# Mean over the rows of an 8192 x 8192 matrix: VectorE additions replaced by fp32 matmuls on four TensorE column tiles, with 4 MB loads on two DMA queues

## The chip, the cores and the metric

The kernel runs on one core of one Trainium2 chip. Its time is the time on the device, in microseconds; each number called a time is the median of several runs. A profile is one execution recorded by the hardware profiler; its span runs from the first to the last instruction.

## The reference

The input is a matrix of 8192 rows and 8192 columns in fp32, 268.4 MB. The output has 8192 elements, the mean of each column:

```python
def reference(x: np.ndarray) -> np.ndarray:
    return np.mean(x, axis=0)
```

There is one addition for each element read, and almost nothing is written.

## The kernel before, in words

The rows lie on the 128 partitions: a row tile is 128 consecutive rows, and there are 64 of them (`n_rt`). The columns are cut into four blocks of 2048 (`CB`, `n_cb`). One load brings one block of one row tile, 128 rows of 8 KB, 1 MB in all.

All loads are issued by SyncE, on its DMA queue, in the order of the loops: row tile by row tile, and in each the four column blocks. The pool `ld` has eight buffers of 1 MB, so up to eight loads are in flight or waiting to be used. The first four loads (line 35) go to the list `firsts`; from row tile 1 on, each load (line 42) is followed by one addition on VectorE. For row tile 1 the addition writes `firsts + t` into one of four accumulators `accs` of 128 x 2048 (line 44); for the other 62 row tiles it adds `t` to the accumulator in place (line 46). So VectorE makes 252 additions of 128 x 2048 fp32 elements, and a buffer is free for the next load when its addition is done.

After that, each accumulator holds 128 partial sums per column. They are summed over the partitions with TensorE: `ones` is a column of 128 elements with the value 1/8192, and `ones.T @ accs` gives a row of 512 means in a PSUM bank (line 52). There are 16 such matmuls, four for each column block. VectorE copies each row from PSUM to SBUF (line 53), and SyncE stores each finished block of 2048 means (line 54). These three lines stand after the loops over the row tiles.

The loads are thus made of rows of 8 KB because a block is 2048 columns wide; in memory a row of the matrix is 32 KB without a gap.

The order of work is that of the program on each engine; a framework puts in the waits between engines (a load waits until its buffer is free, an addition waits for its load, and so on). An fp32 matmul call shows in the trace as two MATMUL instructions, each with a weight load (LDWEIGHTS) of its own.

Of the kernel before, what the change touches and what calls it, by code (L numbers as in the profile page):

```python
# [1 line left out]

# [4 lines left out]


@with_exitstack
def kernel(  # L10
    ctx: ExitStack,
    tc: tile.TileContext,
    x: bass.AP,
    out: bass.AP,
):
    nc = tc.nc
    M, N = x.shape
    P = nc.NUM_PARTITIONS
    CB = 2048
    n_cb = (N + CB - 1) // CB  # L20
    n_rt = (M + P - 1) // P
    FREE = nc.PSUM_BANK_SIZE_BYTES // 4

    with tc.tile_pool(name="ld", bufs=8) as ld, \
         tc.tile_pool(name="acc", bufs=1) as accp, \
         tc.tile_pool(name="sg", bufs=1) as sg, \
         tc.tile_pool(name="psum", bufs=4, space=bass.MemoryType.PSUM) as psp, \
         tc.tile_pool(name="res", bufs=2) as resp:
        ones = sg.tile([P, 1], mybir.dt.float32)
        nc.any.memset(ones[:], 1.0 / M)  # L30
        accs = [accp.tile([P, CB], mybir.dt.float32, name=f"acc{i}") for i in range(n_cb)]
        firsts = []
        for cb in range(n_cb):
            t0 = ld.tile([P, CB], mybir.dt.float32)
            nc.sync.dma_start(out=t0[:], in_=x[0:P, cb * CB:(cb + 1) * CB])  # L35
            firsts.append(t0)
        for ri in range(1, n_rt):
            r0 = ri * P
            for cb in range(n_cb):
                c0 = cb * CB  # L40
                t = ld.tile([P, CB], mybir.dt.float32)
                nc.sync.dma_start(out=t[:], in_=x[r0:r0 + P, c0:c0 + CB])  # L42
                if ri == 1:
                    nc.vector.tensor_add(out=accs[cb][:], in0=firsts[cb][:], in1=t[:])  # L44
                else:
                    nc.vector.tensor_add(out=accs[cb][:], in0=accs[cb][:], in1=t[:])  # L46
        for cb in range(n_cb):
            c0 = cb * CB
            r = resp.tile([1, CB], mybir.dt.float32)
            for fi in range(0, CB, FREE):  # L50
                ps = psp.tile([1, FREE], mybir.dt.float32)
                nc.tensor.matmul(out=ps[:], lhsT=ones[:], rhs=accs[cb][:, fi:fi + FREE])  # L52
                nc.vector.tensor_copy(out=r[:, fi:fi + FREE], in_=ps[:])  # L53
            nc.sync.dma_start(out=out[c0:c0 + CB], in_=r[:1, :])


# [1 line left out]
_INS = ['x']  # L58
_OUTS = [((8192,), 'float32')]


# [23 lines left out]
```

## Time and profile before

| what | value |
|---|---|
| time, median of 3 runs | 659.93 us (659.87 to 660.07) |
| span of the profiled execution | 658.1 us |
| VectorE busy | 587.1 us, 268 instructions |
| TensorE busy (matmul) | 17.0 us, 32 instructions |
| loads | 256 of 1024 KB, issued by SyncE, median 17.5 us from issue to landing |
| read from HBM | 268.44 MB, 408 GB/s over the span |

The profile of the execution gives its span; the runs' times also contain what lies around it, 1.83 us by the difference of the two numbers above. Engines are named PE (TensorE matmul), PEld (TensorE weight load), DVE (VectorE), ACT (ScalarE), POOL (GpSimd) and SP (SyncE). `L46` is line 46 of the listing. A row of a group reads: line, engine, operation, output <- input with their shapes, then the count, the busy time in us, the mean of one in ns, and after the bar the idle time before these instructions and what ended it. In the chain that ended last, a row is start (us from the span's start), duration, and what it was. In a row of windows, each engine has its busy time and number of instructions in that stretch, then follow the clock that TensorE was granted, the mean busy share of the 16 DMA engines, and what they moved in GB/s. `q1` is the queue that carries the loads and stores; `q14` brings the engines their instructions.

### The profile page before, as it was taken

The numbers are of one execution on the slowest core, as the hardware profiler recorded it, in microseconds if no ns is written. First come the engines' busy times: TensorE is split into PE (matmuls) and PEld (weight loads), VectorE is DVE, ScalarE is ACT, GpSimd is POOL, SyncE is SP. The second block draws the span as 40 slices with busy tenths as digits, with TensorE's granted clock in tenths as the row PEclk, the third lists the DMA queues.
The fourth block names the chain that finished last, engine by engine and source line by source line (L and its number), as shares of the span: only waits on it lengthen the run. The fifth ranks groups of instructions, "written<-read, shape, count | busy, mean of one in ns | idle before, by whom it ended". The sixth has DMA issues, their size and how long they took to land.

```text
span 658.1 us, 1142 instructions
## 1 busy us (share of the span) xinstructions
PE 17.0 (3%) x32; PEld 2.8 (0%) x32; DVE 587.1 (89%) x268; POOL 0.3 (0%) x5
## 2 busy tenths in 40 slices
PE   0000000000000000000000000000000000000028
PEld 0000000000000000000000000000000000000001
DVE  0999989999999998999999999899999999899997
POOL 0000000000000000000000000000000000000000
PEclk9999999999999999999999999999999999999999
DMA  8999999999999999999999999999999999999980
GB/s 366 422 422 422 422 421 421 421 423 421 422 422 422 422 421 421 421 422 422 422 422 422 422 422 422 419 422 421 421 422 422 422 422 422 421 421 421 422 349 2
DMA packets 36880, 268.55 MB, mean 408 GB/s; under 512 B 4100, under 2 KB 4100, under 8 KB 4100
## 3 DMA queue, kind: packets, MB, share of 16 engines
q1 hardware_dynamic: 36872, 268.48, 98.1%
q14 instruction: 8, 0.07, 0.0%
HBM read 268.44 MB, written 0.03 MB: 408 GB/s over the span
## 4 chain that ended last, share of the span: by engine, by line
DMA 85%; DVE 12%; PE 1%; issue 1%; SPq 0%; DVEq 0%
DMA t<-in_x_dram 85%; DVE acc L46 12%; PE ps L52 1%; DVE acc L44 0%; DVE r L53 0%; SPq L35 0%; DVEq L46 0%; SPq L42 0%; DVEq L44 0%
## 5 line engine op out<-in xcount | busy, mean ns | idle before, releaser
L46 DVE TENSOR_TENSOR acc<-acc,t 128x2048 f32<-128x2048 f32 x248 | 568.0, 2292 | 51.4 <-DMA t<-in_x_dram 51.4
L52 PE MATMUL ps<-acc,ones 128*1 128x512 f32 x32 | 17.0, 691 | 638.0 <-DVE acc L46 637.9
L44 DVE TENSOR_TENSOR acc<-t,t 128x2048 f32<-128x2048 f32 x4 | 9.2, 2292 | 16.1 <-DMA t<-in_x_dram 16.1
L53 DVE COPY r<-ps 1x512 f32<-1x512 f32 x16 | 10.3, 673 | 1.0 <-PE ps L52 0.9
L52 PEld LDWEIGHTS ps<-acc,ones 128*1 128x1 f32 x32 | 2.8, 91 | 651.2 <-issue 646.5
L69 POOL MEMSET const-bfloat16-1.0<- 128x1 bf16 x1 | 0.1, 101 | 0.0
L69 POOL MEMSET const-uint8-127<- 128x1 uint8 x1 | 0.1, 101 | 0.0
L30 POOL MEMSET ones<- 128x1 f32 x1 | 0.1, 98 | 0.3 <-POOLq L69 0.3
L69 POOL MEMSET const-float32-0.0<- 128x1 f32 x1 | 0.1, 98 | 0.2 <-issue 0.2
L69 POOL MEMSET const-float32-1.0<- 128x1 f32 x1 | 0.1, 98 | 0.0
## 6 DMA issues: line engine op xcount, KB each, us to landing
t<-in_x_dram SPq DMA_DIRECT2D x256, 1024.0 KB, 17.5
out_dram<-r SPq DMA_DIRECT2D x4, 8.0 KB
```

The costliest lines, as they stand in the source:

```text
L30: nc.any.memset(ones[:], 1.0 / M)
L44: nc.vector.tensor_add(out=accs[cb][:], in0=firsts[cb][:], in1=t[:])
L46: nc.vector.tensor_add(out=accs[cb][:], in0=accs[cb][:], in1=t[:])
L52: nc.tensor.matmul(out=ps[:], lhsT=ones[:], rhs=accs[cb][:, fi:fi + FREE])
L53: nc.vector.tensor_copy(out=r[:, fi:fi + FREE], in_=ps[:])
L69: nc = _bacc.Bacc("TRN2", target_bir_lowering=False, num_devices=1)
```

## The change

All additions move from VectorE to TensorE. `ones` becomes a block of 128 x 32 with the value 1/8192. The 8192 columns of a row tile are cut into 16 pieces of 512; each piece is multiplied with `ones` and accumulated in PSUM over all 64 row tiles. Four PSUM banks hold the sums (`NB` = 4). In each bank a piece has 32 of the 128 partitions, all 32 with the same sums, and the matmul that writes it uses the column tile of TensorE at the same place: 128 rows by 32 columns of the array (`tile_position=(0, 32 * q)`). The program goes through the four column tiles in turn.

A load is now a whole row tile, 128 rows of 32 KB, 4 MB. The pool `ld` has five such buffers. Even row tiles are issued by SyncE, odd ones by ScalarE, each on its own DMA queue.

The last row tile is loaded in seven pieces by SyncE, into buffers of its own: three of 1 MB, one for each of the first three banks, and four of 256 KB (runs of 512 B) for the last bank. When a bank has its last matmul, VectorE copies the bank (128 x 512) to SBUF and ScalarE stores one partition of each group of 32.

The core of the diff:

```diff
-    CB = 2048
-        ones = sg.tile([P, 1], mybir.dt.float32)
-                nc.sync.dma_start(out=t[:], in_=x[r0:r0 + P, c0:c0 + CB])
-                    nc.vector.tensor_add(out=accs[cb][:], in0=accs[cb][:], in1=t[:])
-                nc.tensor.matmul(out=ps[:], lhsT=ones[:], rhs=accs[cb][:, fi:fi + FREE])
-                nc.vector.tensor_copy(out=r[:, fi:fi + FREE], in_=ps[:])
-            nc.sync.dma_start(out=out[c0:c0 + CB], in_=r[:1, :])
...
+    F = 512
+    NB = N // (4 * F)
+    n_rt = M // P
+    SPL = 128
...
+    ld = ctx.enter_context(tc.tile_pool(name="ld", bufs=5))
+    lastp = ctx.enter_context(tc.tile_pool(name="lastp", bufs=1))
...
+    ones = sg.tile([P, 32], f32)
+    nc.vector.memset(ones[:], 1.0 / M)
+    banks = [psp.tile([P, F], f32, name=f"bank{b}") for b in range(NB)]
+
+    def mm(b, q, c0, w, rhs, start, stop):
+        nc.tensor.matmul(
+            out=banks[b][32 * q:32 * q + 32, c0:c0 + w],
+            lhsT=ones[:],
+            rhs=rhs,
+            start=start,
+            stop=stop,
+            tile_position=(0, 32 * q),
+            skip_group_check=True,
+        )
+
+    for ri in range(n_rt - 1):
+        t = ld.tile([P, N], f32)
+        (nc.sync if ri % 2 == 0 else nc.scalar).dma_start(out=t[:], in_=x[ri * P:(ri + 1) * P, :])
+        for b in range(NB):
+            for q in range(4):
+                c = (b * 4 + q) * F
+                mm(b, q, 0, F, t[:, c:c + F], ri == 0, False)
+
+    r0 = (n_rt - 1) * P
+    out_v = out.rearrange("(b q c) -> b q c", b=NB, q=4)
+    x_v = x.rearrange("r (b q c) -> r b q c", b=NB, q=4)
+    for b in range(NB - 1):
+        t = lastp.tile([P, 4, F], f32, name=f"last{b}")
+        nc.sync.dma_start(out=t[:], in_=x_v[r0:r0 + P, b])
+        for q in range(4):
+            mm(b, q, 0, F, t[:, q, :], False, True)
+        r = resp.tile([P, F], f32, name=f"r{b}")
+        nc.vector.tensor_copy(out=r[:], in_=banks[b][:])
+        nc.scalar.dma_start(out=out_v[b], in_=r[0:128:32, :])
+    b = NB - 1
+    r = resp.tile([P, F], f32, name=f"r{b}")
+    for s in range(F // SPL):
+        t = lastp.tile([P, 4, SPL], f32, name=f"lasts{s}")
+        nc.sync.dma_start(out=t[:], in_=x_v[r0:r0 + P, b, :, s * SPL:(s + 1) * SPL])
+        for q in range(4):
+            mm(b, q, s * SPL, SPL, t[:, q, :], False, s == F // SPL - 1)
+    nc.vector.tensor_copy(out=r[:], in_=banks[b][:])
+    nc.scalar.dma_start(out=out_v[b], in_=r[0:128:32, :])
```

More of the change, by code (lines that the diff above doesn't have):

```diff
@@ L16 @@
     nc = tc.nc
+    f32 = mybir.dt.float32
     M, N = x.shape
     P = nc.NUM_PARTITIONS
-    CB = 2048
[L20 to L28, printed above, removed]
-        ones = sg.tile([P, 1], mybir.dt.float32)
[L30 to L41, printed above, removed]
-                nc.sync.dma_start(out=t[:], in_=x[r0:r0 + P, c0:c0 + CB])
[L43 to L53, printed above, removed]
-            nc.sync.dma_start(out=out[c0:c0 + CB], in_=r[:1, :])
@@ new lines @@
+    F = 512
[4 more added lines that the diff above has]
+    lastp = ctx.enter_context(tc.tile_pool(name="lastp", bufs=1))
+    sg = ctx.enter_context(tc.tile_pool(name="sg", bufs=1))
+    psp = ctx.enter_context(tc.tile_pool(name="psum", bufs=1, space=bass.MemoryType.PSUM))
+    resp = ctx.enter_context(tc.tile_pool(name="res", bufs=1))
+    ones = sg.tile([P, 32], f32)
+    nc.vector.memset(ones[:], 1.0 / M)
+    banks = [psp.tile([P, F], f32, name=f"bank{b}") for b in range(NB)]
```

## The prediction

> **What bounds the kernel now.** I read the page first (engines, slices, packets), then the chain in order of time, then windows over the last 20 us.
>
> ```profile
> span 658.1 us, 1142 instructions
> ...
> DMA  8999999999999999999999999999999999999980
> ...
> DMA packets 36880, 268.55 MB, mean 408 GB/s; under 512 B 4100, under 2 KB 4100, under 8 KB 4100
> ...
> q1 hardware_dynamic: 36872, 268.48, 98.1%
> q14 instruction: 8, 0.07, 0.0%
> ...
> DMA 85%; DVE 12%; PE 1%; issue 1%; SPq 0%; DVEq 0%
> L46 DVE TENSOR_TENSOR acc<-acc,t 128x2048 f32<-128x2048 f32 x248 | 568.0, 2292 | 51.4 <-DMA t<-in_x_dram 51.4
> L52 PE MATMUL ps<-acc,ones 128*1 128x512 f32 x32 | 17.0, 691 | 638.0 <-DVE acc L46 637.9
> ```
>
> The 16 DMA engines are full until the last two slices. VectorE is busy for 568 us, but what it idles for is the next load. The stream sets the time, then an end in which no load runs. The pace of the stream:
>
> ```profile
> 600.47 17.47 DMA t<-in_x_dram
> ...
> 618.02 2.30 DVE acc L46
> ...
> 620.35 17.48 DMA t<-in_x_dram
> ```
>
> A load of eight in flight takes 17.47 us, and the next on the same buffer starts 19.88 after the one before: 2.485 us per 1 MB. Four stretches of the chain, 160 us apart, are longer:
>
> ```profile
> 79.98 18.12 DMA t<-in_x_dram
> ...
> 239.66 18.43 DMA t<-in_x_dram
> ...
> 399.66 18.43 DMA t<-in_x_dram
> ...
> 559.72 18.45 DMA t<-in_x_dram
> ```
>
> They exceed 17.47 by 0.65 + 0.96 + 0.96 + 0.98 = 3.55 us. The page has 8 packets of instructions, two for each of these; I take them as the cause. What they leave is seen where the stream ends:
>
> ```profile
> core 0: us, PE busy (x) PEld busy (x) DVE busy (x) POOL busy (x), PEclk, DMA share, GB/s
> 637.00:638.00 1.00, 0.14 (x1) 0.11 (x2) 0.81 (x2) 0.00 (x0) 1.00 1.04 434
> 638.00:639.00 1.00, 1.00 (x2) 0.13 (x1) 1.00 (x1) 0.00 (x0) 1.00 0.48 197
> 639.00:640.00 1.00, 1.00 (x2) 0.13 (x1) 1.00 (x1) 0.00 (x0) 1.00 0.12 49
> 641.00:642.00 1.00, 1.00 (x2) 0.13 (x1) 1.00 (x1) 0.00 (x0) 1.00 0.10 41
> 642.00:644.00 2.00, 2.00 (x4) 0.34 (x3) 2.00 (x3) 0.00 (x0) 1.00 0.00 0
> 656.68:656.70 0.02, 0.00 (x0) 0.00 (x0) 0.00 (x0) 0.00 (x0) 1.00 0.03 0
> ```
>
> One engine moves 1 MB / 16 per 2.485 us, 26.4 GB/s, so 49 GB/s are two engines: two of 16 work on for three microseconds after the rest, as if each fetch always falls to the same engine of its queue. The stream is over at about 642.3.
>
> ```profile
> 15.52 2.29 DVE L44 TENSOR_TENSOR acc<-t,t 128x2048 f32<-128x2048 f32 x1 [15.52 <-DMA t<-in_x_dram]
> ...
> 654.97 0.68 DVE L53 COPY r<-ps 1x512 f32<-1x512 f32 x1 [0.18 <-PE ps L52]
> ```
>
> The first add needs five loads: 15.52 - 5 x 2.485 puts the start at 3.1. Check: 3.1 + 256 x 2.485 + 3.55 = 642.8. After the stream come 15.8 us of matmuls and copies in turn; from the end of the last copy (655.65) to the end of the span, 2.45. The median of the runs, 659.93, is 1.83 above the profiled span; I keep that.
>
> **The stream after the change.** Each engine now moves, per 4 MB, 8 rows of 32 KB and one small completion packet, where it moved 32 rows of 8 KB and four (the 4100 small packets are 256 x 16 and 4). The last window above holds only the completion packet of the last store: 3% of 16 engines x 0.02 us is 9.6 ns, nearly all of it fixed cost. If each packet carries that, a row tile saves (24 + 3) x 9.6 = 0.26 us: 9.94 becomes 9.68, and 63 tiles take 609.8. If rows are still cut at 8 KB, only the three small packets go, 0.03 per tile. I take the first: before, too, a row of the tile was one packet. The last row tile: three loads of 1 MB, 7.46, and four of 256 KB in runs of 512 B. A run is a sixteenth of a packet's bytes ((2485 - 9 x 9.6) / 8 / 16 = 18.7 ns) + 9.6; 32 of them and a completion make 0.92, four 3.7. Sum: 3.1 + 609.8 + 7.5 + 3.7 = 624.0, before fetches.
>
> The second queue shares the same engines, and the share is at 1.0 already, so I give it nothing. SyncE issues 39 transfers in place of 260, ScalarE, otherwise idle, 35. A load that waits for its buffer has only later loads of its queue behind it, and four others are in flight: 0, as long as TensorE is less than three tiles (29 us) behind. The 252 adds vanish; they lay beside the stream: 0.
>
> **Fetching TensorE's program.** This part is new. A call of matmul is four instructions (16 calls: 32 MATMUL and the weight loads below). The changed kernel has 63 x 16 + 12 + 16 = 1036 calls, 4144 instructions. 1142 instructions went with 8 packets, 143 each, so 29 packets. What one costs the path: 3.55 / 8 = 0.44 us, if both fetches of a stretch delay the same engine; 0.89, if each has its own, as the two late engines say; 0, if TensorE's fetches spread over 16 engines. I take 0.44, the mean of the ends and the price per packet that the path shows, since a second data queue may fill part of the gap: 12.8 us. SyncE's and VectorE's own 3.55 go (few instructions are left there); the 624.0 does not hold them.
>
> [...]
>
> **TensorE's pace.**
>
> ```profile
> 641.23 0.13 PEld L52 LDWEIGHTS ps<-acc,ones 128*1 128x1 f32 x1 [0.73 <-issue]
> 642.08 0.13 PEld L52 LDWEIGHTS ps<-acc,ones 128*1 128x1 f32 x1 [0.73 <-issue]
> ...
> 644.22 0.08 PEld L52 LDWEIGHTS ps<-acc,ones 128*1 128x1 f32 x1 [0.34 <-issue]
> 644.65 0.08 PEld L52 LDWEIGHTS ps<-acc,ones 128*1 128x1 f32 x1 [0.34 <-issue]
> ```
>
> Half a matmul takes 0.85 us for the first six microseconds, then 0.43 (the clock column says 1.00 throughout; I go by the pace). So 0.86 per call, 13.7 per row tile of 16: over the 9.7 of its load. All hangs on overlap between the column tiles, which nothing here shows. In program order, the second half of a call waits for the first on its tile, and the next call's first half can run beside it: two at a time, 0.43 per call, 6.9 per row tile. All four at once: 3.4. Either hides under the stream. I take the pairs, since the halves come in order in the rows.
>
> [...]
>
> **The end.** Two queues that take turns on each engine land two tiles together: 60 and 61, then 62, then the last row. From the first landing TensorE has 16 x 3 + 12 + 4 = 64 calls' work, 27.5 us, and 3 more for its slow start; the stream has one tile and the last row, 9.7 + 11.2, and a fetch: 21.3. So TensorE ends 9.2 after the stream (0.9 with four at once). Then wait and copy (0.18 + 0.68, the same 512 columns) and 2.45: 3.3.
>
> **Forecast.** 624.0 + 12.8 + 9.2 + 3.3 = 649.3; + 1.8 = 651 us, 1.3% faster. Its own range, with a fetch at 0.3 to 0.7 and either overlap, is 639 to 658.
>
> **The rivals.**
> - Fetches cost nothing on the path, because they spread over the engines or fall into gaps: 624.0 + 9.7 + 3.3 + 1.8 = 639, down to 630 with four column tiles at once. For it: TensorE fetched nothing during the stream of this trace, so its own way of fetching is not shown. Against: both engines that did fetch paid. 0.23. [...]
> - Slower: one DMA engine carries all of TensorE's fetches at 0.89, 25.8 us; every load waits for that engine. 624.0 + 25.8 + 8.8 + 3.3 + 1.8 = 664. It decides against the change from (658.1 - 624.0 - 12.5) / 29 = 0.74 us per packet. For it: the two late engines; against: in front of two queues the gap may be smaller. 0.20.
> - Rows still go in 8 KB pieces: 14.5 us come back, 666. 0.08.
> - The change does not do what it says, the column tiles run one after another: 64 x 13.7 from 22.5 (two tiles landing together) with a slow start and the end is about 909. 0.11.
>
> **How the numbers follow.** The forecast has 0.36; 0.02 is left for turns between two queues costing time, which one queue cannot show. A measurement here tells 0.2% (1.3 us) from no change. Faster: the forecast but for its edge, and the first rival, 0.57. Same: the edges of forecast and second rival, 0.06. Slower: the rest, 0.37. The range 630 to 667 leaves out the serial case, the queue turns and the outer ends.
>
> **What would show it.** Packets: a mid-stream rate of about 430 GB/s (4.19 MB per 9.68 us), and 63 x 128 = 8064 packets of 32 KB. Fetches: q14 with some 29 more packets, and near the end of the stream windows at 26 or so GB/s, one engine alone, for 10 us or more. Overlap: row tiles' matmuls 6.9 us apart in warm stretches (3.4 or 13.7 refute it). The end: a last wait of the copy on TensorE, not on a load. A share of DMA under 0.95 in mid-stream would make the whole sum wrong: then the buffers, hence TensorE, set the pace.

## The result, and the profile after

The changed kernel takes 634.22 us (median of 4 runs, 634.12 to 634.25), beside 659.97 us for the kernel before (4 runs, 659.87 to 660.07). The ratio is 0.961, with a 95% interval of 0.9597 to 0.9624: 3.9% faster. Forecast were 651 us and 1.3%. The direction and the range held; the gain came out three times as large.

The page of the changed kernel, the lines that answer to those of before:

```profile
span 632.4 us, 4331 instructions
...
PE 292.3 (46%) x2072; PEld 71.7 (11%) x2072; DVE 2.9 (0%) x5; POOL 0.2 (0%) x4
...
PEclk9967776578766787766787658786668865687669
DMA  8999999999999999999999999999999999999996
GB/s 375 439 437 430 433 430 431 433 428 431 428 433 430 433 431 432 431 432 431 431 430 431 428 431 431 430 431 428 433 431 430 433 432 431 431 430 431 432 426 234
DMA packets 11664, 268.73 MB, mean 425 GB/s; under 512 B 1136, under 2 KB 3184, under 8 KB 3200
...
q1 hardware_dynamic: 7152, 138.41, 51.2%
q10 hardware_dynamic: 4496, 130.06, 47.9%
q8 instruction: 16, 0.26, 0.2%
```

The stream is still the bound: the DMA engines are full to the last slice but one (9 tenths or more from the second slice on). It moves about 431 GB/s where it moved 422, with 11,664 packets in place of 36,880. TensorE is busy for 46% of the span. The packets of instructions come on q8, 16 of 16 KB (0.26 MB); the prediction had reckoned with 29 packets of 8 KB on q14. The clock that TensorE was granted, 1.00 in the windows of before, is now 0.743 in the mean of the span, and between 0.50 and 1.00 in the windows of the last section.

The chain at the end, in order of time, and the windows of the same stretch:

```profile
578.89 39.23 DMA t<-in_x_dram
...
621.59 7.01 DMA lasts<-in_x_dram
...
628.64 0.47 PE bank L43 x8
...
629.13 0.69 DVE r L79
```

```profile
622.00:624.00 2.00, 1.49 (x16) 0.16 (x8) 0.69 (x1) 0.00 (x0) 1.00 1.11 356
624.00:626.00 2.00, 0.48 (x8) 0.16 (x8) 0.69 (x1) 0.00 (x0) 1.00 0.89 265
626.00:628.00 2.00, 1.51 (x28) 0.46 (x23) 0.69 (x1) 0.00 (x0) 1.00 0.56 167
628.00:629.00 1.00, 0.74 (x16) 0.27 (x16) 0.00 (x0) 0.00 (x0) 1.00 0.04 12
```

The stream is over at 628.6, and 0.47 us of matmuls, one copy and the store follow: 3.8 us to the end of the span. Before, the stream was over at 642.3 and 15.8 us followed. So of the 25.7 us of span, 13.7 come from the stream and 12.0 from the end. The windows show the rate falling off over some six microseconds, where the prediction expected one engine alone at 26 GB/s for ten or more.

TensorE's matmuls in time, rows chosen over the run, with the idle time before each in brackets:

```profile
22.65 9.66 PE L43 MATMUL bank<-t,ones 128*32 128x512 f32 x64 [22.65 <-DMA t<-in_x_dram]
41.98 8.53 PE L43 MATMUL bank<-t,ones 128*32 128x512 f32 x64 [9.68 <-DMA t<-in_x_dram]
62.85 10.04 PE L43 MATMUL bank<-t,ones 128*32 128x512 f32 x64 [12.33 <-DMA t<-in_x_dram]
82.28 8.86 PE L43 MATMUL bank<-t,ones 128*32 128x512 f32 x64 [9.40 <-DMA t<-in_x_dram]
...
295.99 9.53 PE L43 MATMUL bank<-t,ones 128*32 128x512 f32 x64 [10.43 <-DMA t<-in_x_dram]
315.42 8.35 PE L43 MATMUL bank<-t,ones 128*32 128x512 f32 x64 [9.90 <-DMA t<-in_x_dram]
...
354.28 9.39 PE L43 MATMUL bank<-t,ones 128*32 128x512 f32 x64 [10.56 <-DMA t<-in_x_dram]
375.21 9.17 PE L43 MATMUL bank<-t,ones 128*32 128x512 f32 x64 [11.53 <-DMA t<-in_x_dram]
...
608.41 8.62 PE L43 MATMUL bank<-t,ones 128*32 128x512 f32 x64 [9.63 <-DMA t<-in_x_dram]
```

64 MATMUL instructions are the 32 calls of two row tiles: two tiles land together, one from each queue, as the prediction had it. From the first burst to the one at 608.41 there are 60 row tiles in 585.8 us, 9.76 each. Most pairs of tiles come 19.43 us apart, that is 9.71 per tile, where 9.68 was forecast; two pairs come some 1.5 us later than that (62.85 and 375.21), which the part on instruction packets takes up. The weight loads within a burst show how the halves overlap (PEld, from the same kernel):

```profile
316.27 0.20 PEld L43 LDWEIGHTS bank<-t,ones 128*32 128x32 f32 x4 [0.66 <-issue]
317.12 0.20 PEld L43 LDWEIGHTS bank<-t,ones 128*32 128x32 f32 x4 [0.66 <-issue]
...
318.87 0.12 PEld L43 LDWEIGHTS bank<-t,ones 128*32 128x32 f32 x4 [0.31 <-issue]
319.30 0.12 PEld L43 LDWEIGHTS bank<-t,ones 128*32 128x32 f32 x4 [0.31 <-issue]
```

Four at a time, 0.85 us apart at first and 0.43 later: in the time of one half (0.43 us each on one column tile, in the experiments), all four column tiles work on one each. The prediction had taken two at a time.

### The profile page after: what moved, and what is told of

Its sections match the earlier page's. It is cut to its first block, busy times and chain, and to the rows that moved or that the text cites. A ratio compares the mean times of both kernels' runs of the same rounds, so it can differ in the third digit from the quotient of the medians.

```text
span 632.4 us, 4331 instructions
## 1 busy us (share of the span) xinstructions
PE 292.3 (46%) x2072; PEld 71.7 (11%) x2072; DVE 2.9 (0%) x5; POOL 0.2 (0%) x4
## 2 busy tenths in 40 slices
DMA packets 11664, 268.73 MB, mean 425 GB/s; under 512 B 1136, under 2 KB 3184, under 8 KB 3200
## 4 chain that ended last, share of the span: by engine, by line
DMA 75%; PE 18%; another core or an unknown queue 5%; SPq 1%; issue 0%; DVE 0%
DMA t<-in_x_dram 74%; PE bank L43 18%; DMA lasts<-in_x_dram 1%; SPq L76 1%; DVE r L79 0%; SPq L55 0%
## 5 line engine op out<-in xcount | busy, mean ns | idle before, releaser
L43 PE MATMUL bank<-t,ones 128*32 128x512 f32 x2016 | 287.8, 735 | 334.0 <-DMA t<-in_x_dram 334.0
L43 PEld LDWEIGHTS bank<-t,ones 128*32 128x32 f32 x2016 | 70.4, 132 | 550.5 <-DMA t<-in_x_dram 339.5
L70 DVE COPY r<-bank 128x512 f32<-128x512 f32 x3 | 2.1, 692 | 624.6 <-PE bank L43 624.6
L43 PE MATMUL bank<-last,ones 128*32 128x512 f32 x24 | 3.2, 600 | 2.0 <-DMA last<-in_x_dram 2.0
L43 PE MATMUL bank<-lasts,ones 128*32 128x128 f32 x32 | 1.7, 282 | 0.7 <-DMA lasts<-in_x_dram 0.6
L79 DVE COPY r<-bank 128x512 f32<-128x512 f32 x1 | 0.7, 691 | 1.5 <-PE bank L43 1.5
```

The costliest lines, as they stand in the source:

```text
L43: nc.tensor.matmul(out=banks[b][32 * q:32 * q + 32, c0:c0 + w], lhsT=ones[:], rhs=rhs, start=start, stop=stop, tile_position=(0, 32 * q), ...
L70: nc.vector.tensor_copy(out=r[:], in_=banks[b][:])
L79: nc.vector.tensor_copy(out=r[:], in_=banks[b][:])
```

## The experiments

Two questions were open. Which part of the change gave the stream its 13.7 us: the size of the packets, the second queue, or the move of the additions off VectorE? And which of the prediction's terms, the instruction packets and the pace of TensorE, was mis-sized, and why? All times are medians beside the kernel before on the same chip, which took 659.8 to 660.1 us in all these runs.

**The second queue.** All row tiles are issued by SyncE.

```diff
-        (nc.sync if ri % 2 == 0 else nc.scalar).dma_start(out=t[:], in_=x[ri * P:(ri + 1) * P, :])
+        nc.sync.dma_start(out=t[:], in_=x[ri * P:(ri + 1) * P, :])
```

> All row-tile loads on SyncE's queue, otherwise the changed kernel (634.2 us). Theory: the stream is faster because a row is one packet of 32 KB and not four of 8 KB; the second queue adds nothing: 634, within 1 us. Rival: the second queue gives rate, by filling the gaps that one queue leaves (at fetches and between loads): up to the 14 us that the stream gained come back, 640 to 648.

Measured: 634.17, 634.38 and 634.52 us in three executions, and 642.57 in a fourth, the profiled one. From its trace, two windows and the end of TensorE's work:

```profile
628.00:629.00 1.00, 1.00 (x8) 0.11 (x4) 0.00 (x0) 0.00 (x0) 1.00 0.03 10
629.00:632.00 3.00, 3.00 (x16) 0.36 (x8) 0.69 (x1) 0.00 (x0) 1.00 0.00 0
```

```profile
598.83 29.07 PE L43 MATMUL bank<-t,ones 128*32 128x512 f32 x96
...
634.78 2.65 PE L43 MATMUL bank<-lasts,ones 128*32 128x128 f32 x32
```

Its stream ends before 629, as in the changed kernel. TensorE takes 1.2 us per group of four (29.07 us for 24 groups), at a granted clock of 1.00 in these windows, and finishes more than 8 us after the stream. Why it was that slow in this one execution stays open. One queue moves the data as fast as two (634.2 to 634.5 us for 634.2): the second adds nothing to the rate.

**The size of a packet.** The tile gets a gap of 16 elements behind each 2048, so that a row is four packets.

```diff
-        t = ld.tile([P, N], f32)
-        (nc.sync if ri % 2 == 0 else nc.scalar).dma_start(out=t[:], in_=x[ri * P:(ri + 1) * P, :])
+        t = ld.tile([P, NB, 4 * F + 16], f32)
+        x_b = x.rearrange("r (b c) -> r b c", b=NB)
+        (nc.sync if ri % 2 == 0 else nc.scalar).dma_start(out=t[:, :, 0:4 * F], in_=x_b[ri * P:(ri + 1) * P, :, :])
...
```

> Loads of 4 MB on two queues as in the changed kernel, but each row of a tile lands as four runs of 8 KB with a gap of 64 B between them in SBUF. Theory: each packet has a fixed cost of about 9.6 ns; 24 more per engine and row tile, 63 tiles: 14.5 us more, 649. Rival: it was the 4 MB loads or the two queues that quickened the stream, not the size of a packet: 634 to 636.

Measured: 645.02 us (644.91 to 645.09), 10.8 more than the changed kernel. From its page:

```profile
GB/s 349 426 424 425 424 423 424 423 424 424 424 424 423 424 425 425 424 423 424 425 423 425 423 426 425 423 426 423 424 425 424 425 423 425 424 423 424 425 424 240
DMA packets 35856, 268.73 MB, mean 418 GB/s; under 512 B 1136, under 2 KB 3184, under 8 KB 3200
```

With 4 MB loads on two queues but packets of 8 KB the rate is back at 424. The size of a packet is the larger part of the stream's gain: 10.8 us for 24 more packets per engine and 63 tiles are 7.1 ns each, where 9.6 was taken. That is 0.17 us of the 0.23 that a row tile saves; the other 0.06 goes with one load in place of four, and no run takes it apart.

**The kernel before with the large loads.** VectorE's additions, one queue and the matmuls at the end stay; a load is a whole row tile.

```diff
-    with tc.tile_pool(name="ld", bufs=8) as ld, \
+    with tc.tile_pool(name="ld", bufs=4) as ld, \
...
-                nc.sync.dma_start(out=t[:], in_=x[r0:r0 + P, c0:c0 + CB])
+            nc.sync.dma_start(out=t[:], in_=x[r0:r0 + P, :])
+            for cb in range(n_cb):
...
+                nc.vector.tensor_add(out=accs[cb][:], in0=in0, in1=t[:, c0:c0 + CB])
```

> The kernel before (VectorE additions, one queue, matmuls at the end) with loads of a whole row tile, 4 MB in rows of 32 KB, in four buffers. Theory: the stream gains what the packets' fixed cost gave, some 15 us, and the end grows by a few us, as four additions follow the last landing in place of one: 645 to 650. Rival: the gain of the stream belongs to TensorE's part or the second queue (VectorE's reads slow the landing, say): 658 or more.

Measured: 651.82 us (651.82 to 652.09). The end of its chain:

```profile
597.19 29.82 DMA t<-in_x_dram
...
627.11 8.90 DVE acc L41 x4
636.00 0.60 DVE r L48
...
636.65 10.47 PE ps L47 x24
```

The last load has landed at 627.0, some 15 us earlier than before, with VectorE still adding. Some 1.6 us of it go with fewer instruction packets (4 on q14, where there were 8): the chain has two stretches that are a microsecond longer than the others (30.81 and 30.82 for 29.84), where before four exceeded theirs by 3.55 in all. So the stream's gain needs neither TensorE nor the second queue. The end is 7.5 us longer (650.3 - 627.0 = 23.3 for 15.8), since four additions follow the last landing; this hid half of the gain, and made the result 2 us slower than expected. What moving the sum to TensorE, with the last row tile in small pieces, buys is the end. How much of it VectorE would reach with small last pieces was not tried.

**Instruction packets.** Each matmul of the 63 row tiles is split into two, in a second kernel into four, over the columns.

```diff
-            for q in range(4):
-                c = (b * 4 + q) * F
-                mm(b, q, 0, F, t[:, c:c + F], ri == 0, False)
+            for h in range(0, F, 256):
+                for q in range(4):
+                    c = (b * 4 + q) * F + h
+                    mm(b, q, h, 256, t[:, c:c + 256], ri == 0 and h == 0, False)
```

> Each matmul of 512 columns of the 63 row tiles is split into two of 256: the same columns through the array, twice the instructions, 16 more instruction packets of 16 KB. Theory: these packets go to the DMA engines in turn, so 16 more at 1.1 to 1.5 us put 1 to 3 us on the most loaded engine: 635 to 637.5. Rival (the prediction's): one engine carries them all: 16 x 1.1 to 1.5, 18 to 24 us more, 652 to 658. Second rival: they are hidden: 634.

> Each matmul of 512 columns of the 63 row tiles is split into four of 128: the same columns, four times the instructions, 48 more instruction packets of 16 KB. Theory (packets in turn over several engines, 1.1 to 1.5 us each): 3 to 9 us on the most loaded engine: 637 to 644. Rival: one engine carries them all: 48 x 1.1 to 1.5, 53 to 72 us: 687 or more. Second rival: hidden, 634.

Measured: 637.29 us (637.19 to 637.34) with twice, 644.34 (643.43 to 645.25) with four times the instructions. The queue that brings them, in the first and in the second:

```profile
q8 instruction: 32, 0.52, 0.3%
```

```profile
q8 instruction: 63, 1.03, 0.7%
```

Sixteen more packets cost 3.07 us, 0.19 each. A packet occupies a DMA engine for about 1 us (0.7% of 16 engines x 641.8 us / 63 = 1.1). Had one engine carried them all, each would have cost the stream at least that, by this estimate, and not 0.19. The run with four times the instructions lies 0.3 us above what was expected: 10.1 us for 47 packets, at most 0.22 each, since TensorE's last bursts also took part in its chain (5.37 us at 627.7 and 4.63 at 633.9).

The rows of TensorE's bursts in the section on the result show where the price falls due. In the changed kernel, with 16 packets, two pairs of row tiles come late, by 1.44 and 1.50 us: nearly the 3.0 us of all its packets. With 32 packets four pairs come late (at 43.4, 200.3, 357.3 and 514.2), by about 1.4 us each. So one pair came late for every eight packets. At the end of the kernel with four times the instructions, four microseconds have about half of the 16 engines' time in use:

```profile
624.00:626.00 2.00, 1.47 (x55) 1.20 (x43) 0.00 (x0) 0.00 (x0) 1.00 0.46 193
626.00:628.00 2.00, 0.32 (x8) 0.32 (x12) 0.00 (x0) 0.00 (x0) 0.95 0.45 184
```

These views do not name the engine of a packet, so why one pair came late for every eight was not shown.

The reverse: VectorE adds each odd row tile up to 59 to the even one, and TensorE takes the sum.

```diff
+        if ri < 60 and ri % 2 == 0:
+            even = t
+            continue
+        if ri < 60:
+            for b in range(NB):
+                s = slice(b * 4 * F, (b + 1) * 4 * F)
+                nc.vector.tensor_add(out=even[:, s], in0=even[:, s], in1=t[:, s])
+            t = even
...
-                mm(b, q, 0, F, t[:, c:c + F], ri == 0, False)
+                mm(b, q, 0, F, t[:, c:c + F], ri == 1, False)
```

> VectorE adds each odd row tile up to 59 to the even one before it (30 x 4 additions of 128 x 2048), and TensorE takes the sum: nearly half as many calls, 8 or so instruction packets in place of 16. Theory: each packet costs 0.19 us as in the runs with more instructions, so 1.5 us less: 632.7. Rival: the 16 packets of the changed kernel do not lie on the path any more: 634.2. Second rival: the additions hold the buffers longer and loads wait: 640 or more.

Measured: 633.28 us (633.13 to 633.69). To be sure of so small a step, it was run again beside the changed kernel on one chip:

> The changed kernel once more, on the same chip as the next one, so that the two can be compared: 634.2.

> The kernel with pairs of row tiles added on VectorE, beside the changed kernel on the same chip. Theory: 8 instruction packets fewer at 0.12 to 0.19 us: 1.0 to 1.5 us under the changed kernel. Rival: the 0.9 us between the two in different runs is a difference between chips: no more than 0.3 us apart.

Measured: 634.19 (634.13 to 634.42) for the changed kernel and 633.34 (633.11 to 633.84) for this one, with `q8` down to 8 packets. The 0.85 us are 0.11 per packet, if all of it is theirs, under the 0.12 that was the lower end. This version is faster than the changed kernel in both comparisons, without an overlap of their times, though by 0.13% only.

**The overlap of the column tiles.** First, all four pieces of a bank on one column tile, then on two. The sums of different pieces mix, so these two kernels do not give the mean.

```diff
-            out=banks[b][32 * q:32 * q + 32, c0:c0 + w],
+            out=banks[b][32 * p:32 * p + 32, c0:c0 + w],
...
-            tile_position=(0, 32 * q),
+            tile_position=(0, 32 * p),
...
```

where `p` is 0 in the one and `q % 2` in the other.

> All four pieces of a bank go through one column tile (the sums of four pieces are mixed and the other partitions of the output are zero, so the output is not the mean; the same matmuls and loads). Theory: it is the column tiles that let matmuls overlap; on one tile a call costs 0.86 us, 13.7 per row tile, and TensorE sets the pace: 895 to 915. Rival: the overlap comes from elsewhere (the two halves of a call, or calls to different banks): under 700.

> The four pieces of a bank go through two column tiles in turn (pieces 0 and 2, 1 and 3 are mixed, the other partitions of the output are zero: not the mean; the same matmuls and loads). This makes the pace that the prediction assumed: 0.43 us per call, 6.9 per row tile. Theory: it still hides under the stream, but TensorE ends some 8 to 9 us after it, as the prediction worked out: 641 to 644. Rival: the lag at the end does not come about, because TensorE's work beside the last loads is hidden: 634 to 636.

Measured: 908.80 us (908.69 to 909.57) on one tile and 652.23 (652.11 to 652.45) on two. The chains:

```profile
22.70 880.69 PE bank L44 x2072
```

```profile
574.29 42.62 DMA t<-in_x_dram
...
616.95 29.35 PE bank L44 x152
...
646.32 0.68 DVE r L82
```

On one tile TensorE works without a break, 2072 halves in 880.7 us, 0.43 each: the column tiles are the whole of the overlap. On two tiles its work hides under the stream until the end, then lags some 18 us behind it, twice as much as expected. Its work after the landing at 616.9 is close to the sum of the prediction (29.35 us; 30.5 were worked out), but the stream had only some 11 us left at that point (no bytes after 627.5), and not 21.3. The reason is in the loads of the last row tile, whose issues have these rows, in the changed kernel and in this one:

```profile
L66 SPq DMA_DIRECT2D last<-in_x_dram x3: 422/427/432, 579.3 to 580.2; - x3
```

```profile
L67 SPq DMA_DIRECT2D last<-in_x_dram x3: 425/425/426, 117.5 to 208.6; - x3
```

Here the pieces of the last row tile were issued between 117 and 293 us, among the other loads and against the order of the program, and the stream ended with a whole row tile. So this run changed the order of the loads beside the column tiles, and its end does not test the prediction's lag; the next kernel, whose pieces come last, does.

Then the changed kernel with the loops over the pieces exchanged, four calls in succession to one column tile:

```diff
-        for b in range(NB):
-            for q in range(4):
+        for q in range(4):
+            for b in range(NB):
```

> The loops over pieces are exchanged: each row tile sends four calls in succession to one column tile, then four to the next; the same calls, in another order. Theory: matmuls start in the order of the program, and only neighbours on different column tiles overlap, so of 32 halves per row tile four pairs overlap, 28 x 0.43 = 12.0 us per row tile, over the 9.7 of its load: TensorE sets the pace, 780 to 820. Rival: TensorE picks what is ready for each column tile from the instructions ahead, so the order of the calls does not matter: 634 to 636.

Measured: 639.84 us (639.79 to 641.44). Neither theory held. A burst in it:

```profile
315.44 17.52 PE L43 MATMUL bank<-t,ones 128*32 128x512 f32 x64 [1.95 <-DMA t<-in_x_dram]
```

The same 64 halves take 17.5 us, not 8.4 and not 24. One after another at 0.43 they would take 27.5, so this is 1.6 at a time over the burst; between 300 and 311 us the weight loads of this kernel come one to three every 0.43 us, two in the mean. That is more overlap than in the first theory (24 us), and less than all four at once. What sets this pace no run shows; the framework may also have put the calls in another order, as it did with the loads in the kernel before. This kernel has about the pace that the prediction took, and its end shows it: matmuls go on until 634.7, 6.1 us after the stream.

**The pieces of the last row tile.** It is loaded whole, as the others.

```diff
-    for ri in range(n_rt - 1):
+    for ri in range(n_rt):
...
-    for b in range(NB - 1):
-        t = lastp.tile([P, 4, F], f32, name=f"last{b}")
...
```

> The last row tile is loaded whole, as the others, on ScalarE's queue, and not in seven pieces. Theory: the stream gets 1.5 us shorter, and after its last landing come 16 calls in place of four small ones, 3.4 us at the full and 6.8 at the slow pace of TensorE, where 0.5 stood: 636 to 640. Rival: the pieces bring nothing, since the last tile's matmuls are short beside the fixed end: 633 to 635.

Measured: 642.71 us (641.94 to 643.07), 8.5 more, beyond what was expected. Its chain:

```profile
578.96 48.95 DMA t<-in_x_dram
...
627.95 9.14 PE bank L42 x64
```

The last two tiles land together and 64 halves follow, 9.1 us in place of 0.5. The small pieces are worth 8.5 us to this kernel.

## Why the prediction was wrong in size, point by point

- **The bound and the packets: right.** The stream sets the time, and larger packets quickened it (431 GB/s, and 424 with packets of 8 KB). The saving per row tile was 0.23 us (9.94 to 9.71), for 0.26: 2.1 us less in all. The fixed cost was read off the smallest packet, as 3% of 16 engines in 0.02 us; with one digit, that is 8 to 11 ns. The 24 packets of 8 KB cost 7.1 each.
- **The second queue at nothing: right.** 634.2 to 634.5 with one.
- **The instruction packets: the first step that failed.** "I take 0.44, the mean of the ends and the price per packet that the path shows", for 29 packets, 12.8 us. The runs show 16 packets at 0.19, 3.0 us. Of the 9.8 us too much, 5.7 are the 13 packets that did not come and 4.0 the price of the others. The step carried over what q14 showed in the trace before, eight packets of 8 KB and 49 GB/s at the end of the stream, to TensorE, whose program comes in packets of 16 KB on q8 (16, 32 and 63 of them as its calls were split): there one pair of row tiles came late, by 1.4 to 1.5 us, for every eight packets. The first rival, "spread over the engines or fall into gaps", was nearer; the slower one, with one engine at 0.89 per packet, is refuted by the 0.19. What the packets cost is 0.5% of the time (3.0 of 634.2 us), and not nothing, as twice the instructions show (3.07 us more).
- **The pace of TensorE: the second step that failed.** "I take the pairs, since the halves come in order in the rows." The calls go to the four tiles in turn, and all four overlap: 3.4 us per row tile at full pace (eight groups, 0.43 apart), not 6.9. That the halves came in order in the trace before, where all calls used the same columns, could not tell what happens between different tiles.
- **The lag at the end: follows from the pace.** 9.2 us were in the sum for pairs, 0.9 beside it for four at once; it was 0.5. For two at a time the reckoning itself holds: the kernel with the exchanged loops has 26.3 us of work from the landing at 608.4 and 20.2 us of stream, where 30.5 and 21.3 were worked out. Most of the difference is the slow start of 3 us, which it does not have (its granted clock is 1.00 from 610 to 628 us).
- **Wait, copy and store: right,** 3.3 us for 3.3.

The sum: 649.3 - 9.8 (instruction packets) - 8.7 (lag) + 2.1 (row tiles) = 632.9, for a span of 632.4. Both failed steps erred to the same side, and each was a choice between two ends that the prediction had named. The serial rival's price, 909, was met to a microsecond by the kernel that makes it so.

## What to carry to other kernels

When a stream of loads is the bound, as here, look at its packets: 24 fewer per engine and row tile were worth 10.8 us. Count the fixed cost per packet (7.1 ns here), make a row of the tile one long run, and do not expect rate from a second queue when the engines are full already (634.2 us with two queues, 634.2 to 634.5 with one). The work that follows the stream was worth nearly as much as the stream's rate (12.0 us and 13.7): what counts is the work left after the last landing, so let the last loads be small and the engine that takes them ahead of the stream. A cost that one engine's queue shows is not yet the cost for another engine (0.44 us per packet taken from q14, 0.19 measured on q8): where the trace before has no such packet, carry both ends of the cost through the sum. And when an experiment changes one thing, look in its trace whether the loads are still issued in the same order.

## What the runs showed of the hardware that was not expected

How far the column tiles overlapped went with the order of the calls: in turn over four tiles, 64 halves take 8.4 to 10.0 us in the rows above; four in succession to one tile, 17.5. In the rows of weight loads above, a burst starts with its groups 0.85 us apart and goes on with 0.43. Windows of the changed kernel over one gap and one burst, with the granted clock (0.56, 0.50 and 1.00) behind the engines' busy times:

```profile
290.00:296.00 6.00, 0.01 (x3) 0.02 (x3) 0.00 (x0) 0.00 (x0) 0.56 1.02 437
296.00:299.00 3.00, 3.00 (x16) 0.78 (x20) 0.00 (x0) 0.00 (x0) 0.50 1.09 470
...
302.00:306.00 4.00, 3.51 (x36) 0.75 (x28) 0.00 (x0) 0.00 (x0) 1.00 1.08 467
```

At 0.50 of the clock 3 us hold 16 halves; at 1.00, 3.5 us hold 36. The bursts in the rows above, after 9.4 to 12.3 idle microseconds (and the first, which no other precedes), take 8.4 to 10.0 us, where 16 groups at 0.43 would take 6.9. With four tiles at once that costs nothing here, because the burst still ends 9.4 us or more before the next pair lands.
